# A third query block under the first norm, unread products between two blocks, and a rotation moved from TensorE to VectorE

## The chip, the cores and the metric

The kernel runs on one core of one Trainium2 chip. The core has a matrix engine (TensorE, in profiles PE, with its weight loads listed apart as PEld), two engines for elementwise work (VectorE, DVE, and ScalarE, ACT), GpSimd (POOL), and SyncE (SP), which issues most of the transfers between memory and the on-chip buffer. Products land in PSUM, which the kernel uses as eight banks of 128 x 512 numbers. The engines run side by side and wait for one another by semaphores. The metric is the time of one execution in device microseconds: the median of three runs is 2041.04 us (2039.53 to 2041.19).

## What is computed

Two transformer blocks on 256 positions of width 2048, all in float32. In outline:

```
# first block
h = rmsnorm(x, g_pre)
q, k, v, z = split(h @ w_in_a)              # 32 heads of 64, 4 key/value heads
o = sliding_window_attention(q, k, v)       # window 128, ALiBi slopes, one sink per head
y = (o * silu(z)) @ w_out_a
x = x + rmsnorm(y, g_post)
# second block
h = rmsnorm(x, attn_norm_g)
c_q, c_kv, k_pe, dq, dk, dv, gates = split(h @ w_in)
q = rmsnorm(c_q) @ w_uq                     # 16 heads: 128 plain and 64 rotated columns
k, v = split(rmsnorm(c_kv) @ w_ukv)
q_rope, k_rope = rope(q[64 columns]), rope(k_pe)
y_mla  = chunked_attention([q, q_rope], [k, k_rope], v)
y_diff = differential_attention(dq, dk, dv)
x = x + (g0 * (y_mla @ w_mla) + g1 * (y_diff @ w_diff)) @ w_out
h = rmsnorm(x, ffn_norm_g)
x = x + (silu(h @ w_gate) * (h @ w_up)) @ w_down
return rmsnorm(x, final_norm_g)
```

The rotation takes a head's 64 columns as two halves x1 and x2 and gives (x1 cos - x2 sin, x2 cos + x1 sin). A norm's factor is one number per position, so the kernel multiplies with weights first and applies the factor to the product.

## The kernel before, in words

Every activation lies with its columns on the 128 partitions and the 256 positions along the row. Each number is cut into a high part and a low part of a shorter type, and a product of a weight tile w (128 x 128) with an activation tile is formed as w_hi times [a_hi | a_lo], 512 columns in one instruction, plus w_lo times a_hi, 256 columns. `gemm(name, m, acts)` makes one block of 128 output columns this way: for 16 activation tiles it issues 8 products of one kind, 16 of the other and again 16 and 8 in turn, into one PSUM bank. `gemm4` makes four blocks together, tile by tile, into two banks of the tag "g" and two of the tag "s"; the second block's first products are made so, since each needs only one tile of h at a time. PSUM has four banks "g", two "s" and two "t".

The weights arrive as float32 chunks of 16 tiles (w_raw, four buffers); for each half chunk ACT writes the high part (line 84) and DVE the low part (line 85), into four buffers each.

The instructions of each engine run in the order in which a planner puts them ahead of time: it walks the program by priority (the order in which the code is written) and gives an engine the first instruction that its own estimate of times takes for ready, so an instruction that waits can be passed by later ones. Instructions that go through `pin` stay behind what was written before them on their engine; matrix products are not pinned.

Work of the attention and the norms is written as generators. `between.tiles(n)` counts weight tiles inside `gemm` and at each tick (after `every` tiles, there twice per block of 16) advances one generator by a step, so its products land between those of the big matrix products.

Around the change:

- First norm. The keys and values of the first block (ps_k in two "g" banks, ps_v in one of the "s" banks) and the query blocks 0 and 1 (the other two "g" banks) are formed from h before its norm is known. `first_norm` squares x_t (ACT, line 252), adds (DVE), forms the sums over partitions by products with a column of ones (`Squares.sums`), takes the root on POOL (`rstd`, line 277), and spreads the factor over partitions by a diagonal matrix times ones (`rows`, line 284); then k_a, v_a and the queries are scaled (`scaled`), which frees the banks. Its four first steps take two squares each; behind block 1 the generator is drained, that is, run to its end. Block 2 needs a "g" bank.
- Between the blocks. The last output block of `w_out_a` is made by `gemm_sum`; then its square, the sums, the root and `rows` follow one another, and nothing else is there for PE. Each tile of x1 is y times the factor plus x (lines 588 and 589, DVE), and is cut into h (lines 235 and 236) for the first `gemm4` of the second block, whose first weights were cut ahead (w_hi_u, w_lo_u).
- Rotation. `rotate(a)` forms a product of a with a constant matrix rot_m (a permutation with signs) in a "t" bank, multiplies it by sin out of PSUM, multiplies a by cos and adds. It is called once for the shared key part kr and twice in each of four groups for q_r; the scores of a group (`attend_m`) wait for it.

Of the kernel before, what the change touches and what calls it, by code (L numbers as in the profile page):

```python
# [12 lines left out]
ALU = mybir.AluOpType  # L13

P = 128
S = 256
# [10 lines left out]
N_CHUNK = N_TILES // CH  # L27

G_PRE, G_POST, G_ATTN, G_Q, G_KV, G_FFN, B_GATE, G_DIFF, N_COLS = 0, 16, 32, 48, 54, 58, 74, 106, 108
C_ID, C_ROT, C_COS, C_SIN, C_DA, C_DM, C_DD, N_CST = 0, 128, 256, 512, 768, 1152, 1536, 1920  # L30


class Weights:
# [134 lines left out]
def block_kernel(ctx, tc, order, w, xt, cols, bc, fg, cst, out):  # L168
# [10 lines left out]
    def unit(name, dt=F32):  # L179
        return up.tile([P, 512], dt, name=name, tag="u", bufs=NU)  # L180
# [4 lines left out]
    def bank(tag):  # L185
        return psum.tile([P, 512], F32, name=f"ps_{tag}", tag=tag, bufs={"g": 4, "s": 2, "t": 2}[tag])

    def half(t, i):
        return t[:, (i % 2) * S:(i % 2) * S + S]
# [78 lines left out]
    def rstd(src, dim, scale=None):  # L268
        n = src.shape[-1]
        t = sm("ms", n)  # L270
        if scale is None:
            nc.vector.tensor_scalar(out=t, in0=src, scalar1=1.0 / dim, scalar2=EPS, op0=ALU.mult, op1=ALU.add)
        else:
            nc.vector.scalar_tensor_tensor(out=t, in0=src, scalar=1.0 / dim, in1=scale, op0=ALU.mult, op1=ALU.mult)
            nc.vector.tensor_scalar(out=t, in0=t, scalar1=EPS, scalar2=None, op0=ALU.add)
        r = sm("rstd", n)
        nc.gpsimd.tensor_tensor(out=r, in0=t, in1=mhalf[:, 0:n], op=ALU.pow)  # L277
        return r

    def rows(r, rb=None):  # L280

        dg = unit("diag")[:, 0:S]
        for tb in range(2):
            nc.vector.tensor_scalar(out=dg[:, tb * P:tb * P + P], in0=ident, scalar1=r[:, tb:tb + 1], scalar2=None,
                                    op0=ALU.mult)
        ps = bank("t")
        mm(ps[:, 0:S], ones, dg, True, True)
        if rb is not None:
            nc.vector.tensor_copy(out=rb, in_=ps[:, 0:S])
        return ps[:, 0:S]  # L290
# [23 lines left out]
            between.tiles(n)  # L314
            run(same, b, opened)

    def gemm(name, m, acts):

        ps = bank("g")
        parts = [(ps, W.take(name, k * P, m * P), acts[k]) for k in range(len(acts))]  # L320
        if len(parts) > HALF:
            runs(parts[:HALF], parts[HALF:], HALF)
        else:
            runs(parts, [], len(parts))
        return ps

    def gemm4(name, ms, acts):

        pp = [bank("g"), bank("g"), bank("s"), bank("s")]
        opened = set()  # L330
        for k in range(len(acts)):
            parts = [(pp[j], W.take(name, k * P, m * P), acts[k]) for j, m in enumerate(ms)]
            same, other = ("hi", "lo") if k % 2 == 0 else ("lo", "hi")
            run(same, parts, opened)
            run(other, parts, opened)
            between.tiles(len(parts))
        return pp

    def gemm_sum(name, m, acts):

# [114 lines left out]
    def first_norm():  # L455
        for i in range(8):
            sq.add(x_t[i])
            if i % 2:
                yield
        nc.vector.tensor_copy(out=r_a, in_=rstd(sq.sums(), D))  # L460
        yield 2
        rows(r_a, rb)
        yield
        for j in range(2):
            scaled(half(k_a, j), ps_k[j], rb)
        for tb in range(2):
            nc.scalar.activation(out=half(v_a, tb), in_=half(ps_v, tb), func=AF.Copy, scale=r_a[:, tb:tb + 1])
        pin(nc.vector.tensor_scalar(out=negsink, in0=sinks, scalar1=-1.0, scalar2=None, op0=ALU.mult))

    def attend_a(j, q, o):  # L470

        kt = j // 8
        heads = (16 * kt + j % 8, 16 * kt + 8 + j % 8)
        negmax, sums, t = sm("negmax"), sm("sums"), sm("tiny")
        p = []
        pp = [bank("s") for _ in range(2)]
        for a, b, n in ((0, P, P), (P, S, S)):
            for e, ps in enumerate(pp):
                rng = slice(64 * e, 64 * e + 64)
                mm(ps[:, a:a + n], q[rng, a:b], k_a[rng, kt * S:kt * S + n], a == 0, a > 0)  # L480
        for e, ps in enumerate(pp):
            slope = 2.0 ** (-8.0 * (heads[e] + 1) / 32)
            bias = unit("bias")[:, 0:384]
            nc.scalar.activation(out=bias, in_=tab_a, func=AF.Copy, scale=8.0 * slope)
            p.append(exps(ps, bias, 0.125, negmax[:, 2 * e:2 * e + 2], sums[:, 2 * e:2 * e + 2],
                          negsink[:, heads[e]:heads[e] + 1]))
        for e in range(2):
            nc.vector.tensor_scalar(out=t[:, 2 * e:2 * e + 2], in0=negmax[:, 2 * e:2 * e + 2],
                                    scalar1=sinks[:, heads[e]:heads[e] + 1], scalar2=None, op0=ALU.add)
        nc.scalar.activation(out=t, in_=t, func=AF.Exp)  # L490
        rec = sm("rec")
        tt(rec, t, sums, ALU.add)
        nc.vector.reciprocal(out=rec, in_=rec)
        for e in range(2):
            nc.scalar.activation(out=p[e][:, 0:P], in_=p[e][:, 0:P], func=AF.Copy, scale=rec[:, 2 * e:2 * e + 1])
            nc.vector.tensor_scalar(out=p[e][:, P:384], in0=p[e][:, P:384], scalar1=rec[:, 2 * e + 1:2 * e + 2],  # L496
                                    scalar2=None, op0=ALU.mult)
        yield
        pts = [transposed(p[e], e == 1) for e in range(2)]
        yield  # L500
        ps = bank("t")
        vs = [v_a[:, tb * S + (2 * kt + e) * 64:tb * S + (2 * kt + e) * 64 + 64] for e in range(2) for tb in range(2)]
        for e in range(2):
            mm(ps[64 * e:64 * e + 64, 0:S], vs[2 * e], pts[e][:, 0:S], True, False)
        for e in range(2):
            mm(ps[64 * e:64 * e + 64, P:S], vs[2 * e + 1], pts[e][:, S:384], False, True)
        nc.scalar.copy(out=o, in_=ps[:, 0:S])
        done.add(j)
# [2 lines left out]
    between.every, between.apart = 4, 1  # L511
    between.add(first_norm())
    o_a = []
    for j in range(16):
        ps = gemm("in_a", j, h)
        if j == 0:
            ps_0 = ps
            continue
        if j == 1:
            between.drain()  # L520
            between.every, between.apart = 8, 3
        for i, b in ((0, ps_0), (1, ps)) if j == 1 else ((j, ps),):
            if i % 2 == 0:
                q, o = unit("q_a"), unit("o_a")
                o_a.append(o)
            scaled(half(q, i), b, rb)
            between.add(attend_a(i, half(q, i), half(o, i)))

    lam = unit("lam")
    nc.gpsimd.dma_start(out=lam, in_=bc[:, 32:544])  # L530
# [45 lines left out]
                      [(unit("w_hi_u", F32R), unit("w_lo_u", F32R)) for _ in range(2)])  # L576
    ps = gemm_sum("out_a", 15, g)
    sq.add(ps[:, 0:S])
    rb = rows(rstd(sq.sums(), D))
    t = half(y2[7], 1)  # L580
    nc.scalar.activation(out=t, in_=ps[:, 0:S], func=AF.Copy, scale=gcol(G_POST, 15))
    y.append(t)
# [21 lines left out]
    rope = unit("rope")  # L604
    nc.scalar.dma_start(out=rope, in_=cst[:, C_COS:C_COS + 512])
    cos, sin = rope[:, 0:S], rope[:, S:]
    rot_m = unit("rot_m")
    rot, tab_m = rot_m[:, 384:512], rot_m[:, 0:384]
    nc.scalar.dma_start(out=rot, in_=cst[:, C_ROT:C_ROT + P])
    nc.scalar.dma_start(out=tab_m, in_=cst[:, C_DM:C_DM + 384])  # L610

    r_2 = const.tile([P, 2], F32, name="r_2")
# [32 lines left out]

    def rotate(a):

        ps = bank("t")
        mm(ps[:, 0:S], rot, a, True, True)
        b = unit("rope_t")[:, 0:S]  # L650
        tt(b, ps[:, 0:S], sin, ALU.mult)
        tt(a, a, cos, ALU.mult)
        tt(a, a, b, ALU.add)

# [325 lines left out]
def _constants():  # L980
    c = np.zeros((P, N_CST), np.float32)
    c[:, C_ID:C_ID + P] = np.eye(P)
    for b in (0, 64):
        for i in range(32):
            c[b + 32 + i, C_ROT + b + i] = -1.0
            c[b + i, C_ROT + b + 32 + i] = 1.0
    inv = np.float32(10000.0) ** (-np.arange(0, 64, 2, dtype=np.float32) / np.float32(64))
    ang = (np.arange(S, dtype=np.float32)[:, None] * inv[None, :]).astype(np.float32)
    for b in range(4):
        c[b * 32:b * 32 + 32, C_COS:C_COS + S] = np.cos(ang).T  # L990
        c[b * 32:b * 32 + 32, C_SIN:C_SIN + S] = np.sin(ang).T
    q = np.arange(P)[:, None]
    k = np.arange(S)[None, :]
    for q0, o, n in ((0, 0, P), (P, P, S)):
        qq, kk = q + q0, k[:, :n]
        dist = qq - kk
        c[:, C_DA + o:C_DA + o + n] = np.where((dist >= 0) & (dist < 128), -dist, -1e30)
        ok = kk // 64 <= qq // 64
        c[:, C_DM + o:C_DM + o + n] = np.where(ok, 0.0, -1e30)
        c[:, C_DD + o:C_DD + o + n] = np.where(ok, -np.abs(dist), -1e30)  # L1000
    return c
# [69 lines left out]
```

## Time and profile before

| | |
|---|---|
| median of three runs | 2041.04 us |
| the profiled execution's own time | 2042.15 us |
| span, first to last instruction | 2040.4 us |
| mean granted TensorE clock | 0.996 |
| PE busy | 2014.4 us (99%) |
| DVE, ACT busy | 1304.3 us (64%), 1071.6 us (53%) |
| moved from and to memory | 364.89 MB, 179 GB/s |

The profile is of one execution. Busy is the time in which an engine executes something; for PE matrix products overlap, so one instruction's length is more than its share of the stream: 16 products of 512 columns follow one another in 3.65 us, though each is listed with about 0.39. A row of a timeline gives start, length, engine, line, what is written and read, and in brackets how long the engine stood idle before it and who released it. "The chain" follows the execution back from its last instruction; in it the lengths add up to the span.

### The profile page before, as it was taken

The page shows a single profiled execution, that of the slowest core. Times are in us where ns is not written, and L with a number is a line of the kernel's source. Part 1 is how long each engine was busy: PE and PEld are TensorE (multiplying, and loading weights), DVE is VectorE, ACT ScalarE, POOL GpSimd, SP SyncE. Part 2 cuts the span into 40 slices and gives each one's busy share as a digit, 9 for nine tenths or more (in the row PEclk, how much of TensorE's full clock was granted, in tenths as well). Part 3 has the DMA queues.
Part 4 walks back from the last instruction along what each step waited for, and adds up shares of the span by engine and source line. Part 5 has one row for each costly group of instructions (what it writes and reads, how often), then busy time and mean ns, then how long its engine had stood idle before and what let it go on. Part 6 is the DMA issues. An engine that isn't in the chain of part 4 may idle for free.

```text
span 2040.4 us, 28289 instructions
## 1 busy us (share of the span) xinstructions
PE 2014.4 (99%) x11290; PEld 1744.5 (85%) x11290; DVE 1304.3 (64%) x2129; ACT 1071.6 (53%) x1818; POOL 19.2 (1%) x25
## 2 busy tenths in 40 slices
PE   7999999999999999999999999999999999999998
PEld 6787888888888888888888888888888888888886
DVE  6768865887766655566575767666666666555543
ACT  6767655656545444455465445464445554444443
POOL 0000000000000000000000000000000000000000
PEclk9999999999999999999999999999999999999999
DMA  7343456353444555545545555545555555555553
GB/s 295 119 152 128 166 186 232 109 186 125 149 159 171 186 186 187 193 171 174 183 166 186 187 193 193 185 173 187 189 193 194 187 186 187 191 220 186 196 196 103
DMA packets 53667, 364.89 MB, mean 179 GB/s; under 512 B 6240, under 2 KB 7136, under 8 KB 10400
## 3 DMA queue, kind: packets, MB, share of 16 engines
q1 hardware_dynamic: 52560, 361.07, 49.5%
q8 instruction: 88, 1.44, 0.3%
q0 software_dynamic: 400, 1.31, 0.2%
q10 hardware_dynamic: 576, 0.72, 0.1%
q14 instruction: 43, 0.35, 0.1%
HBM read 360.98 MB, written 2.10 MB: 178 GB/s over the span
## 4 chain that ended last, share of the span: by engine, by line
PE 96%; DVE 1%; ACT 1%; issue 1%; DMA 0%; SPq 0%; POOL 0%; POOLq 0%; ACTq 0%; DVEq 0%
PE ps_g L195 89%; PE ps_s L195 5%; PE ps_t L195 2%; PE ps_t L412 1%; DMA w_raw<-w 0%; ACT prob L404 0%; DVE w_lo L85 0%; ACT w_hi L84 0%; PE ps_t L810 0%; PE ps_t L906 0%; POOL rstd L277 0%; PE ps_t L786 0%; DVE prob L400 0%; DVE prob L496 0%; SPq L217 0%
## 5 line engine op out<-in xcount | busy, mean ns | idle before, releaser
L85 DVE TENSOR_TENSOR w_lo<-w_raw,w_hi 128x1024 fp32r<-128x1024 f32 (+1 forms) x676 | 825.6, 1222 | 320.0 <-ACT w_hi L84 289.9
L84 ACT CAST w_hi<-w_raw 128x1024 fp32r<-128x1024 f32 (+1 forms) x676 | 708.3, 1048 | 352.7 <-PE ps_g L195 269.6
L195 PE MATMUL ps_g<-h,w_hi 128*128 128x512 f32 x3064 | 750.1, 393 | 8.1 <-ACT w_hi L84 6.7
L195 PEld LDWEIGHTS ps_g<-h,w_hi 128*128 128x128 f32 x3064 | 561.9, 189 | 120.2 <-ACT w_hi L84 6.7
L195 PEld LDWEIGHTS ps_g<-h,w_lo 128*128 128x128 f32 x3064 | 395.2, 191 | 20.3 <-issue 4.0
L195 PE MATMUL ps_g<-h,w_lo 128*128 128x256 f32 x3064 | 408.4, 284 | 0.9 <-DVE k_a L198 0.9
L195 PE MATMUL ps_g<-w_hi,act 128*128 128x512 f32 x704 | 216.8, 389 | 0.0
L195 PEld LDWEIGHTS ps_g<-w_hi,act 128*128 128x128 f32 x704 | 132.1, 188 | 27.5
L381 ACT COPY ffn<-ps_g 128x256 f32<-128x256 f32 x86 | 31.8, 373 | 200.9 <-PE ps_g L195 200.9
L195 PE MATMUL ps_g<-w_lo,act 128*128 128x512 f32 x352 | 136.9, 389 | 0.0
L198 DVE TENSOR_TENSOR ffn<-ffn,ps_g 128x256 f32<-128x256 f32 x86 | 36.0, 421 | 144.4 <-ACT ffn L381 144.4
L195 PE MATMUL ps_g<-w_hi,h 128*128 128x512 f32 x256 | 79.4, 389 | 0.0
L195 PEld LDWEIGHTS ps_g<-w_lo,act 128*128 128x128 f32 x352 | 66.1, 188 | 13.7
L404 ACT ACTIVATE prob<-prob,negmax 128x128 f32<-128x128 f32 (+1 forms) x128 | 56.7, 445 | 24.1 <-DVE negmax L400 23.5
L195 PE MATMUL ps_g<-y_m,w_hi 128*128 128x512 f32 x256 | 63.8, 391 | 0.0
L195 PE MATMUL ps_g<-y_d,w_hi 128*128 128x512 f32 x256 | 61.2, 391 | 0.0
L195 PE MATMUL ps_g<-g,w_hi 128*128 128x512 f32 (+1 forms) x240 | 57.8, 377 | 0.0
L195 PEld LDWEIGHTS ps_g<-w_hi,h 128*128 128x128 f32 x256 | 48.1, 188 | 9.9
L195 PE MATMUL ps_g<-mg,w_hi 128*128 128x512 f32 x224 | 56.0, 391 | 0.0
L195 PEld LDWEIGHTS ps_g<-y_d,w_hi 128*128 128x128 f32 x256 | 47.0, 188 | 9.1
L195 PEld LDWEIGHTS ps_g<-y_m,w_hi 128*128 128x128 f32 x256 | 47.0, 188 | 9.1
L195 PE MATMUL ps_g<-c,w_hi 128*128 128x512 f32 x208 | 53.6, 400 | 0.0
(238 smaller groups left out, 1859.2 us busy)
## 6 DMA issues: line engine op xcount, KB each, us to landing
w_raw<-w SPq DMA_DIRECT2D x337, 1024.0 KB, 4.8
w_raw<-w SPq DMA_DIRECT2D x5, 512.0 KB, 7.8
out<-x2n SPq DMA_DIRECT2D x8, 256.0 KB, 3.1
x_t<-xt SPq DMA_DIRECT2D x7, 256.0 KB, 7.8
fgt<-fg POOLq DMA_DIRECT2D x4, 256.0 KB, 5.5
w_raw<-w SPq DMA_DIRECT2D x2, 256.0 KB, 4.6
x_t<-xt SPq DMA_DIRECT2D x2, 128.0 KB, 3.2
lam<-bc POOLq DMA_DIRECT2D x1, 256.0 KB, 6.1
```

The source lines that it names most:

```text
L84: a = nc.scalar.copy(out=hi[:, q], in_=src[:, q])
L85: b = nc.vector.tensor_tensor(out=lo[:, q], in0=src[:, q], in1=hi.bitcast(F32)[:, q], op=ALU.subtract)
L195: nc.tensor.matmul(out=o, lhsT=a, rhs=b, start=start, stop=stop, skip_group_check=True)
L198: nc.vector.tensor_tensor(out=o, in0=a, in1=b, op=op)
L381: nc.scalar.copy(out=o, in_=ps[:, S:])
L404: nc.scalar.activation(out=t[:, a:b], in_=t[:, a:b], func=AF.Exp, scale=-1.0, bias=negmax[:, qb:qb + 1], accum_out=sums[:, qb:qb + 1])
L412: nc.tensor.transpose(out=ps[:, j * P:j * P + P], in_=p[:, j * P:j * P + P], identity=ident)
```

## The change

Three edits.

- The first norm's generator takes four squares per step instead of two, and the loop over query blocks makes block 2 as well before draining it; block 2 is written into an "s" bank. All three blocks are scaled, and their attention queued, behind block 2.
- `busy(n, cols)` issues n products of g[0] with itself, cols columns wide, into an "s" bank that nothing reads. It is called three times between the blocks: 8 of 128 columns after the sums, 2 of 256 after the root, 8 of 512 after `rows`.
- `rotate` uses no product: for each group of 32 partitions, DVE multiplies a by sin and writes the result to the neighbouring group (q ^ 32). The sign of the rotation is in the table of sin, the matrix rot_m and its load are gone.

```
     def first_norm():
         for i in range(8):
             sq.add(x_t[i])
-            if i % 2:
+            if i % 4 == 3:
                 yield
...
+    early = []
     for j in range(16):
-        ps = gemm("in_a", j, h)
-        if j == 0:
-            ps_0 = ps
+        ps = gemm("in_a", j, h, "s" if j == 2 else "g")
+        early.append((j, ps))
+        if j < 2:
             continue
-        if j == 1:
+        if j == 2:
             between.drain()
             between.every, between.apart = 8, 3
-        for i, b in ((0, ps_0), (1, ps)) if j == 1 else ((j, ps),):
+        for i, b in early:
             if i % 2 == 0:
                 q, o = unit("q_a"), unit("o_a")
                 o_a.append(o)
             scaled(half(q, i), b, rb)
             between.add(attend_a(i, half(q, i), half(o, i)))
+        early = []
...
+    def busy(n, cols):
+
+        ps = bank("s")
+        for _ in range(n):
+            mm(ps[:, 0:cols], g[0][:, 0:P], g[0][:, 0:cols], True, True)
...
     sq.add(ps[:, 0:S])
-    rb = rows(rstd(sq.sums(), D))
+    sums = sq.sums()
+    busy(8, P)
+    r = rstd(sums, D)
+    busy(2, S)
+    rb = rows(r)
+    busy(8, 512)
...
-    rot_m = unit("rot_m")
-    rot, tab_m = rot_m[:, 384:512], rot_m[:, 0:384]
-    nc.scalar.dma_start(out=rot, in_=cst[:, C_ROT:C_ROT + P])
+    tab_m = unit("tab_m")[:, 0:384]
...
     def rotate(a):
 
-        ps = bank("t")
-        mm(ps[:, 0:S], rot, a, True, True)
         b = unit("rope_t")[:, 0:S]
-        tt(b, ps[:, 0:S], sin, ALU.mult)
+        for q in range(0, P, 32):
+            tt(b[q ^ 32:(q ^ 32) + 32], a[q:q + 32], sin[q:q + 32], ALU.mult)
         tt(a, a, cos, ALU.mult)
         tt(a, a, b, ALU.add)
...
-        c[b * 32:b * 32 + 32, C_SIN:C_SIN + S] = np.sin(ang).T
+        c[b * 32:b * 32 + 32, C_SIN:C_SIN + S] = np.sin(ang).T * (1.0 if b % 2 == 0 else -1.0)
```

More of the change, by code (lines that the diff above doesn't have):

```diff
@@ L29 @@
 G_PRE, G_POST, G_ATTN, G_Q, G_KV, G_FFN, B_GATE, G_DIFF, N_COLS = 0, 16, 32, 48, 54, 58, 74, 106, 108
-C_ID, C_ROT, C_COS, C_SIN, C_DA, C_DM, C_DD, N_CST = 0, 128, 256, 512, 768, 1152, 1536, 1920
+C_ID, C_COS, C_SIN, C_DA, C_DM, C_DD, N_CST = 0, 128, 384, 640, 1024, 1408, 1792
 class Weights:
@@ L315, in runs, with gemm @@
             run(same, b, opened)
-    def gemm(name, m, acts):
-        ps = bank("g")
+    def gemm(name, m, acts, tag="g"):
+        ps = bank(tag)
         parts = [(ps, W.take(name, k * P, m * P), acts[k]) for k in range(len(acts))]
@@ L982, in _constants @@
     c[:, C_ID:C_ID + P] = np.eye(P)
[L983 to L986, printed above, removed]
     inv = np.float32(10000.0) ** (-np.arange(0, 64, 2, dtype=np.float32) / np.float32(64))
```

## The prediction

> **What bounds the kernel now.** I read the page's busy times first, then PE's share of the waits, then a table of busy time by stretch, and last the instructions around the places where PE stands still.
>
> ```profile
> PE 2014.4 (99%) x11290; PEld 1744.5 (85%) x11290; DVE 1304.3 (64%) x2129; ACT 1071.6 (53%) x1818; POOL 19.2 (1%) x25
> ```
>
> PE is the bound: 26 us of the span of 2040.4 are not PE's. So only two kinds of edit pay: work taken off PE, and the few waits of PE shortened. Its waits behind other engines, apart from the start, are these:
>
> ```profile
> PE ps_t L195 <- DVE diag L284: 4.3, 2, 2.7
> PE ps_g L195 <- DVE h L236: 3.7, 2, 2.2
> PE ps_g L195 <- DVE k_a L198: 0.9, 1, 0.9
> ```
>
> The stretches that the change touches (columns: length, then busy us and instructions of PE, PEld, DVE, ACT, POOL, then the granted clock, DMA share, GB/s):
>
> ```profile
> 33.50:50.00 16.50, 12.90 (x75) 11.15 (x74) 11.06 (x18) 8.02 (x13) 1.54 (x1) 0.99 0.63 235
> 50.00:75.00 25.00, 24.42 (x147) 19.76 (x147) 18.66 (x61) 17.20 (x49) 0.00 (x0) 0.94 0.26 96
> 75.00:200.00 125.00, 124.68 (x770) 99.28 (x769) 87.98 (x246) 85.53 (x222) 0.70 (x1) 1.00 0.41 146
> 352.00:368.00 16.00, 11.97 (x58) 10.09 (x57) 9.47 (x27) 4.59 (x10) 0.72 (x1) 0.68 0.11 33
> 395.00:450.00 55.00, 55.00 (x311) 48.06 (x310) 46.22 (x95) 34.64 (x66) 2.91 (x3) 1.00 0.50 180
> 450.00:600.00 150.00, 150.00 (x877) 128.44 (x876) 111.50 (x253) 85.03 (x188) 0.00 (x0) 1.00 0.41 146
> ```
>
> The reader is to see two holes of PE (16.50 - 12.90 = 3.6 us and 16.00 - 11.97 = 4.0 us), each with a granted clock below 1 in or behind it, and no hole at all in the two stretches where the rotations lie.
>
> **First norm: the third query block.** PE's own instructions there (start, length, what; in brackets the idle time before):
>
> ```profile
> 40.04 3.82 PE L195 MATMUL ps_g<-h,w_hi 128*128 128x512 f32 x16
> 43.69 1.12 PE L195 MATMUL ps_g<-h,w_lo 128*128 128x256 f32 x8
> 44.65 0.50 PE L195 MATMUL ps_t<-ones,sq 128*128 128x1 f32 x4
> 47.81 0.70 PE L195 MATMUL ps_t<-diag,ones 128*128 128x256 f32 x2 [2.66 <-DVE diag L284]
> 49.45 1.86 PE L195 MATMUL ps_g<-h,w_lo 128*128 128x256 f32 x8 [0.94 <-DVE k_a L198]
> 51.10 2.46 PE L195 MATMUL ps_g<-h,w_hi 128*128 128x512 f32 x6
> 53.50 0.93 PE L195 MATMUL ps_s<-k_a,q_a 64*128 64x128 f32 x8
> ```
>
> Blocks 0 and 1 end at 44.65; then sums, root, diagonal and k_a must finish before block 2 gets a ps_g bank. That is 2.66 + 0.94 = 3.6 us of idle. Behind it PE runs slow: 8 low-half products take 51.10 - 49.45 = 1.65 us against 44.65 - 43.69 = 0.96 before, and 6 high-half ones 53.50 - 51.10 = 2.40 against 6 x (43.69 - 40.04)/16 = 1.37. That is 0.69 + 1.03 = 1.7 us lost to the clock, so 5.3 us in all.
>
> With the change, sums fall a quarter into block 1 (about 40), rows a quarter into block 2 (about 46), k_a at its third quarter. Block 2 writes a ps_s bank, which is free because ps_v holds only one of two, and runs 5.6 us (3.65 + 2 x 0.96) through what was the hole. The chain from sums to rows was 47.81 - 44.65 = 3.2 us, against the two ticks of 2.8 us, half a block, that it now has, so it is hidden; k_a's adds free the ps_g bank before block 3 asks for it. Moved with it: the squares are two per tick more, on ACT and DVE, which are busy 8.0 and 11.1 of 16.5 us here. The first attention now starts one block later with three heads' pairs queued instead of two, and waits for block 2's own scaling to free its second ps_s bank, much as it waited four us (49.45 to 53.50) before. No DMA is moved past another. I take -5.2; bounds -3.6 (the idle alone, the clock falls elsewhere) and -5.5.
>
> **Between the blocks: products nobody reads.**
>
> ```profile
> 354.75 1.24 PE L195 MATMUL ps_t<-ones,sq 128*128 128x1 f32 x8
> 357.64 1.22 PE L195 MATMUL ps_t<-diag,ones 128*128 128x256 f32 x2 [1.65 <-DVE diag L284]
> 361.11 1.19 PE L195 MATMUL ps_g<-h,w_hi_u 128*128 128x512 f32 x2 [2.25 <-DVE h L236]
> ```
> ```profile
> 368.29 0.24 PE ps_g L195 x2
> 371.07 0.24 PE ps_g L195 x2
> 382.25 0.24 PE ps_g L195 x2
> ```
> ```profile
> 379.23 0.48 DVE L236 SCALAR_TENSOR_TENSOR h<-y,colt,h 128x256 fp32r<-128x256 f32 x1
> ```
>
> The first fence is PE's timeline, the second the chain that ended last. The rows product takes 1.22 us where the first norm's took 0.70: the clock is already down. The first three k steps of the new block take 368.29 - 361.11 = 7.18 us; two later ones take 371.07 - 368.29 = 2.78, so three cost 4.17 at full clock: 3.0 us lost, of which I leave 0.3 for filling the pipe.
>
> The change adds, on PE alone, 8 products of 128 columns before the root, 2 of 256 behind it, 8 of 512 behind rows. A 256-column one costs 0.12 (0.96/8), a 512-column one 0.23 (3.65/16). A 128-column one of this type is not in the trace; 4 products of one column took 0.50, so the bounds are 0.12 and the 0.23 of four times the width, and I take 0.12, the nearer row by shape. So 1.0 + 0.24 us fit the gap of 1.65 before rows, and 1.8 the gap of 2.25 behind it. Nobody reads their bank, so nothing waits for them except PE's own next instruction.
>
> If the clock holds, rows takes 0.5 less and everything behind it moves up; and of the 2.7 us behind 361.11 nearly all returns. What is late next: h. Block 13 of h is done at 379.23 + 0.48 and PE begins that step at 382.25, a slack of 2.5 us; PE gains 3.2 on it while DVE gains 0.5, so some 0.2 to 0.4 of the gain is lost there. 0.5 + 2.3 = 2.8; I take off 0.3 because what holds the dummies in place is only the planner:
>
> ```profile
> L817 DVE TENSOR_SCALAR hb<-colt x1: 175/175/175, 3.3 to 3.3; 128x32 f32<-128x32 f32 x1
> ```
>
> This instruction of line 817 ran at 3.3 us: work that is ready is issued early when its engine looks free. I take -2.5; bounds -3.3 and +1.5 (rival 1).
>
> [...]
>
> **Rotation on DVE.** Removed: a product per rotation, and a 64 KB load on ACT's queue. Added: four multiplies of 32 partitions for one of 128.
>
> ```profile
> 454.17 0.87 PE ps_t L195 x4
> ```
> ```profile
> 358.90 0.42 DVE L588 TENSOR_TENSOR y<-y,ps_t 128x256 f32<-128x256 f32 x1 [1.31 <-PE ps_t L195]
> 359.35 0.42 DVE L589 TENSOR_TENSOR y<-y,x_t 128x256 f32<-128x256 f32 x1
> 359.69 0.41 DVE L588 TENSOR_TENSOR y<-y,ps_t 128x256 f32<-128x256 f32 x1
> ```
> ```profile
> 454.01 1.03 PE L195 MATMUL ps_t<-q_r,rot_m 128*128 128x256 f32 x4
> 455.91 0.42 DVE L198 TENSOR_TENSOR rope_t<-ps_t,rope 128x256 f32<-128x256 f32 x1
> 458.25 0.42 DVE L198 TENSOR_TENSOR q_r<-q_r,rope_t 128x256 f32<-128x256 f32 x1
> 459.08 0.93 PE L195 MATMUL ps_s<-rb_kr,q_r 64*128 64x128 f32 x8
> ```
> ```profile
> 490.01 1.03 PE L195 MATMUL ps_t<-q_r,rot_m 128*128 128x256 f32 x4
> 491.37 0.42 DVE L198 TENSOR_TENSOR rope_t<-ps_t,rope 128x256 f32<-128x256 f32 x1
> 493.71 0.42 DVE L198 TENSOR_TENSOR q_r<-q_r,rope_t 128x256 f32<-128x256 f32 x1
> 495.94 0.93 PE L195 MATMUL ps_s<-rb_kr,q_r 64*128 64x128 f32 x8
> ```
>
> Two rotations hold PE 0.87 us, so nine hold it 9 x 0.435 = 3.9, in stretches where PE has no hole: a gain one for one. A multiply of 32 partitions is not in the trace; it streams the same 256 elements per partition as the 0.42 us rows, which I take (bounds 0.1, a quarter, and 0.45, the start-to-start of a dependent pair, 358.90 to 359.35; an independent one follows after 0.34). Three more at 0.42 are 1.26 per rotation, 11.3 for nine. Cover: DVE idles 55.00 - 46.22 + 150.00 - 111.50 = 47.3 us there. What could be late is q_r for the scores. A group of two rotations gets 2.5 us longer on DVE, but need not wait for PE, behind whose start rope_t began 1.9 and 1.4 us later. In the first group q_r was done 459.08 - 458.67 = 0.4 us ahead of the scores, in the second 1.8 us: late by 0.2, and not at all. I allow 0.4 for all four and take -3.5; bounds -3.9 and rival 3. The load removed leaves ACT's queue where ACT waits for DVE anyway, 4.11 us as its next row has it: nothing.
>
> ```profile
> 359.81 0.51 ACT L235 ACTIVATE h<-y,colt 128x256 fp32r<-128x256 f32 x1 [4.11 <-DVE y L589]
> ```
>
> [...]
>
> **Sum.** -5.2 - 2.5 - 3.5 = -11.2 us against the profiled execution's own time of 2042.15 (span 2040.4 and 1.75 around it), so 2031.0. The median of the runs, 2041.04, lies 1.1 below that execution: 2029.8, so 2030. By the bounds the same case reaches from -12.7 to -8.0: 2028 to 2033. About 0.2%, 4.1 us, is what a measurement of this kernel can tell from no change.
>
> **Rivals.** (1) The dummies don't do it. Either the planner issues all eighteen ahead of rows: 1.0 + 0.24 + 1.8 = 3.0 us into the 1.65 us hole makes rows 1.4 late, and the hole behind it stays; or the clock falls all the same, and the eight wide ones at twice 0.23 fill 3.7 us where 2.25 were free, 1.4 late too; or the planner puts them into busy PE time earlier, +3.0. Then this part is +1.4 to +3.0 instead of -2.5: 2033.7 to 2035.3. For it: the row of line 817. Against: ahead of 354.75 PE has no idle place to tempt the planner. (2) The first norm's wait only moves, behind block 2, to the attention's ps_s banks: 5.2 are lost, 2035. For it: scores started 4.0 us after block 2 did. Against: block 3 needs no ps_s bank and can run meanwhile. (3) The other side: q_r comes late in the four groups and DVE becomes what PE waits for. The place is the scores; the price is up to 2.5 us per group, and from 1.65 us on (the shortest hole behind which the clock was down) 3.0 more for the clock. In all four: 4 x 5.5 = 22 us for the rotation's gain, -7.7 - 3.9 + 22 = +10.4, 2051. In two of four: 2040.4, no change. For it: the first group's slack of 0.4 us. Against: the 47 us of idle DVE, and that PE's order lets other products pass the scores, as at 51.10 where six went ahead.
>
> **How the numbers follow.** Forecast 0.58; rival 1 0.2; rival 2 0.07; rival 3 in two groups 0.08, in all 0.07. The first three are faster: 0.85; the others 0.08 the same and 0.07 slower. From 2027.5 (the bound, with the spread of the runs) to 2036.5 lie the first three.
>
> **What would show it.** After the change PE should wait for no diagonal and no k_a near 45 to 50; the granted clock of the first 75 us should be 1; rows between the blocks should take 0.70, and its k steps 1.39 from the first on. No ps_t product from rot_m, 36 DVE multiplies of 32 partitions at about 0.42, and scores right behind. I am wrong if the stretch from the sums to the first k step grows beyond its 6.4 us, if PE's busy share in the rotation stretches falls below all, or if the dummies stand somewhere else.

## The result and the profile after

The changed kernel took 2034.28 us (median; 2033.72 to 2036.05) against 2040.80 us for the kernel before on the same chip: a ratio of 0.997 [0.9961, 0.998], 6.5 us less. The profiled execution took 2034.21 us with a span of 2032.4, 8.0 less than the span before; the profiled execution of before (2042.15) had lain 1.35 us above the median of 2040.80, which is most of the difference between 8.0 and 6.5.

PE is busy for 2010.5 us after, DVE for 1316.0. The waits of PE in the changed kernel (what waited, at what, behind whom: us in total, times, the longest):

```profile
...
PE ps_g L195 <- DVE k_n L198: 1.8, 2, 1.4
PE ps_t L418 <- ACT prob_t L421: 0.8, 1, 0.8
PE ps_s L195 <- DVE negmax L406: 0.7, 2, 0.4
PE ps_t L195 <- DVE diag L284: 0.6, 1, 0.6
PE ps_s L195 <- DVE q_r L198: 0.5, 1, 0.5
```

The wait for k_a is gone and that for the diagonals has shrunk from 4.3 to 0.6 us, as forecast. But waits for k_n, prob_t, negmax and q_r have come up, 3.8 us together. Of these 0.3 us, for negmax at 161 us, lie in the first block, where the kernel before had short waits for prob_t and q_a; the other 3.5 are in the second block and new there. The table by stretch (length, then busy us and count of PE, PEld, DVE, ACT, POOL, then clock, DMA share, GB/s) says where:

```profile
33.50:50.00 16.50, 16.50 (x96) 14.48 (x95) 12.95 (x24) 7.95 (x13) 0.70 (x1) 1.00 0.65 238
50.00:75.00 25.00, 25.00 (x158) 20.57 (x158) 20.02 (x60) 19.36 (x53) 0.00 (x0) 1.00 0.35 131
...
395.00:450.00 55.00, 53.46 (x303) 46.55 (x303) 45.42 (x92) 31.09 (x53) 2.91 (x3) 1.00 0.50 184
450.00:600.00 150.00, 147.86 (x859) 125.47 (x858) 119.55 (x273) 84.08 (x186) 0.00 (x0) 1.00 0.41 144
```

The first hole is closed, at full clock. In the two stretches of the rotations, where PE had no hole before, it now stands still for 1.54 + 2.14 = 3.7 us. PE's timeline at the first norm shows the new order, sums and rows inside blocks 1 and 2, with no idle time ahead of any of them:

```profile
39.41 0.50 PE L195 MATMUL ps_t<-ones,sq 128*128 128x1 f32 x4
...
45.44 0.59 PE L195 MATMUL ps_t<-diag,ones 128*128 128x256 f32 x2
45.68 4.00 PE L195 MATMUL ps_s<-h,w_hi 128*128 128x512 f32 x16
```

and between the blocks:

```profile
349.45 0.50 PE L195 MATMUL ps_t<-ones,sq 128*128 128x1 f32 x4
349.81 0.42 PE L195 MATMUL ps_s<-g 128*128 128x128 f32 x2
...
350.55 1.15 PE L195 MATMUL ps_s<-g 128*128 128x128 f32 x8
352.34 0.70 PE L195 MATMUL ps_t<-diag,ones 128*128 128x256 f32 x2 [0.64 <-DVE diag L284]
352.69 2.20 PE L195 MATMUL ps_s<-g 128*128 128x512 f32 x8
355.20 0.73 PE L195 MATMUL ps_g<-h,w_hi_u 128*128 128x512 f32 x2 [0.31 <-DVE h L236]
```

The 18 unread products stand where they were written (two slipped between the sums; the row of eight at 350.55 is the other six of 128 columns and the two of 256), rows is back at 0.70 us, and the first pair of k-step products takes 0.73 where it took 1.19. The first query block's first products are needed as a mark too, before and after:

```profile
33.51 1.12 PE L195 MATMUL ps_g<-h,w_lo 128*128 128x256 f32 x8
```
```profile
32.88 1.12 PE L195 MATMUL ps_g<-h,w_lo 128*128 128x256 f32 x8
```

The last output's transfers serve as the end mark. They start on SP's queue, before and after:

```profile
2028.80 7.23 SPq L973 DMA_DIRECT2D out<-x2n  x8
```
```profile
2021.30 7.21 SPq L983 DMA_DIRECT2D out<-x2n  x8
```

These marks split the gain. Up to the first query block: 33.51 to 32.88, -0.6; this is start-up and no part of the change (PE leaves its last start-up wait at 15.12 before and 14.49 after). From there to the sums between the blocks: 354.75 - 33.51 = 321.24 to 349.45 - 32.88 = 316.57, -4.7 (first norm). Sums to the first k step: 361.11 - 354.75 = 6.36 to 355.20 - 349.45 = 5.75, -0.6 (mostly rows). From the first k step to the transfers: 1667.7 to 1666.1, -1.6. From there to the end the span shrank by another 0.5, which the runs did not look into. The -1.6 is the disappointment: it should hold the clock's gain for the k steps, about 2.3, and the rotation's 3.5.

The instructions in which PE resumes after an idle time in the rotation stretches:

```profile
426.10 0.48 PE L195 MATMUL ps_g<-w_hi,c 128*128 128x512 f32 x1 [1.41 <-DVE k_n L198]
...
453.22 0.50 PE L195 MATMUL ps_g<-w_hi,c 128*128 128x512 f32 x1 [0.44 <-DVE k_n L198]
...
454.23 0.93 PE L195 MATMUL ps_s<-rb_kr,q_r 64*128 64x128 f32 x8 [0.50 <-DVE q_r L198]
...
503.12 1.02 PE L418 MATMUL ps_t<-ident,prob 128*128 128x128 f32 x6 [0.83 <-ACT prob_t L421]
...
527.53 1.58 PE L195 MATMUL ps_s<-k_n,q_n 128*128 128x128 f32 x8 [0.37 <-DVE negmax L406]
```

Only one of the five waits is for a rotated tile q_r. What delays the longest is told by the chain of that stretch:

```profile
423.80 0.42 DVE rope_t L198
...
424.22 0.41 DVE rope_t L198
...
424.65 0.42 DVE rope_t L198
...
425.08 0.42 DVE rope_t L198
...
425.53 0.42 DVE k_n L198
```

The four multiplies of kr's rotation run on DVE immediately ahead of the k_n that empties a "g" bank, and PE waits for that k_n with its next product into a "g" bank. How that stood with the product is seen in the first experiment.

### The profile page after: what moved, and what is told of

Read it like the earlier page. It is cut to its first block, busy times and chain, and to the rows that moved or that the text cites. A ratio compares the mean times of both kernels' runs of the same rounds, so it can differ in the third digit from the quotient of the medians.

```text
span 2032.4 us, 28308 instructions
## 1 busy us (share of the span) xinstructions
PE 2010.5 (99%) x11290; PEld 1740.7 (86%) x11290; DVE 1316.0 (65%) x2156; ACT 1071.9 (53%) x1818; POOL 18.3 (1%) x25
## 4 chain that ended last, share of the span: by engine, by line
PE 95%; DVE 2%; ACT 1%; DMA 1%; issue 1%; POOL 0%; SPq 0%; ACTq 0%; POOLq 0%; DVEq 0%
PE ps_g L195 87%; PE ps_s L195 5%; PE ps_t L195 2%; PE ps_t L418 1%; DMA w_raw<-w 1%; DVE rope_t L198 1%; DVE w_lo L85 1%; DVE k_n L198 0%; ACT w_hi L84 0%; DVE q_r L198 0%; DVE prob L406 0%; PE ps_t L916 0%; PE ps_t L820 0%; POOL rstd L277 0%; PE ps_t L796 0%
```

## Experiments

The kernels start from the changed one unless it is said otherwise, and all compute the whole result. Beside each median stands its ratio to the kernel before, timed in the same job. "The stretch" is from the first k step to the last output's transfers: 1667.7 us before, 1666.1 changed.

**Undo the rotation.**

```
-        for q in range(0, P, 32):
-            tt(b[q ^ 32:(q ^ 32) + 32], a[q:q + 32], sin[q:q + 32], ALU.mult)
+        ps = bank("t")
+        mm(ps[:, 0:S], rot, a, True, True)
+        tt(b, ps[:, 0:S], sin, ALU.mult)
```

> The changed kernel with one part undone: the rotation is a product with rot_m on PE again. Theory T, from the two traces: the rotation on DVE took 3.9 us of products off PE and gave back more in waits, about 1.1 us net, so this kernel takes 2034.3 - 1.1 = 2033.2 us. Rival R, the prediction's own term: the rotation gained 3.5 us and the shortfall lies in another part, so 2037.8 us.

2033.88 us, 0.9962 [0.995, 0.9975]; 0.4 below the changed kernel by the medians, within what the intervals allow, and 1.1 by the stretch, 355.47 to 2020.45 = 1665.0. The table by stretch shows PE without a hole again:

```profile
395.00:450.00 55.00, 55.00 (x313) 48.18 (x312) 45.72 (x93) 31.60 (x53) 2.91 (x3) 1.00 0.53 191
450.00:600.00 150.00, 150.00 (x873) 128.28 (x872) 109.31 (x245) 83.98 (x185) 0.00 (x0) 1.00 0.40 142
```

DVE's timeline at kr, with the product:

```profile
423.96 0.42 DVE L198 TENSOR_TENSOR rope_t<-ps_t,rope 128x256 f32<-128x256 f32 x1
...
424.62 0.41 DVE L198 TENSOR_TENSOR k_n<-k_n,ps_g 128x256 f32<-128x256 f32 x1
```

The rotation stood ahead of k_n here too, but k_n starts 0.66 us after rope_t; in the chain of the changed kernel it is 425.53 - 423.80 = 1.73, and PE, with a product less to make, comes for the bank earlier. So the rotation on DVE, as placed, brought nothing and by the profile cost 1.1 us; with the product back the stretch is 2.7 shorter than before, and since the rotations are then as before, that is put down to the clock in the k steps.

**Undo the unread products.**

```
-    sums = sq.sums()
-    busy(8, P)
-    r = rstd(sums, D)
-    busy(2, S)
-    rb = rows(r)
-    busy(8, 512)
+    rb = rows(rstd(sq.sums(), D))
```

> The changed kernel without the eighteen unread products. Theory T: between the end of the last output block and the fourth k step of the second block the changed kernel is 3.3 to 3.5 us shorter, and that is the granted clock, so without the products the clock is down again behind the gap and the time is 2037.7 us, with a rows product of 1.2 us. [...]

2036.5 us, 0.9975 [0.9965, 0.9986]: 2.2 more than the changed kernel, 2.1 by the stretch (355.21 to 2023.38 = 1668.2). PE's timeline and the table by stretch:

```profile
352.26 0.70 PE L195 MATMUL ps_t<-diag,ones 128*128 128x256 f32 x2 [1.65 <-DVE diag L284]
355.21 1.19 PE L195 MATMUL ps_g<-h,w_hi_u 128*128 128x512 f32 x2 [2.25 <-DVE h L236]
```
```profile
352.00:354.00 2.00, 0.70 (x2) 0.30 (x2) 1.17 (x5) 0.09 (x1) 0.00 (x0) 0.71 0.12 45
354.00:356.00 2.00, 0.79 (x2) 0.72 (x3) 1.93 (x6) 1.04 (x3) 0.00 (x0) 0.50 0.00 0
356.00:358.00 2.00, 2.00 (x8) 1.71 (x8) 1.93 (x6) 0.91 (x2) 0.00 (x0) 0.50 0.00 0
358.00:360.00 2.00, 2.00 (x9) 1.77 (x9) 1.97 (x6) 1.02 (x2) 0.00 (x0) 0.58 0.00 0
```

The same two holes as before the change, and the clock falls, but later against the work: rows runs at 0.70, and only the k steps are slow. Of the 3.3 us that this boundary gained in the profiles (0.6 + 2.7), the unread products hold 2.1; the other 1.2 is there without them, in this profile and with the boundary some 5 us earlier than before the change.

**Undo the third block.** Two blocks ahead of the drain, two squares per step, block 2 in a "g" bank.

```
-            if i % 4 == 3:
+            if i % 2:
...
-        ps = gemm("in_a", j, h, "s" if j == 2 else "g")
+        ps = gemm("in_a", j, h)
...
-        if j < 2:
+        if j < 1:
             continue
-        if j == 2:
+        if j == 1:
```

> The changed kernel with two query blocks before the first norm is drained and two squares per step, as before. Theory T: the last output block of the first transformer block ended 5.3 us earlier with three blocks, and all of it is kept, so 2039.6 us. Rival: a part of it is given back behind, where three heads' pairs of attention start together; then 2037 us or less.

2039.04 us, 0.9988 [0.998, 0.9997]: 4.8 more than the changed kernel, 4.9 by the span of 2037.3. The hole is the old one (PE is busy for 12.90 of the 16.50 us from 33.50 on), and the clock is down to 0.50 behind it (50 to 52 us). From the first query block, at 33.12, to the sums, at 354.36, it takes 321.24 us, as in the kernel before; so the third block is worth 4.7.

This kernel also shows the unread products at nearly the old place of the boundary:

```profile
357.25 0.70 PE L195 MATMUL ps_t<-diag,ones 128*128 128x256 f32 x2 [0.63 <-DVE diag L284]
```

The kernel before, with its sums at 354.75 and no such products, had 1.22 for this row. From the sums to the first k step (360.11) it is 5.75 us here, and the stretch is 2026.15 - 360.11 = 1666.0, both as in the changed kernel. Against the kernel before that is 0.6 + 1.7, and with the 1.1 that the rotation costs, 3.4: in this place the products are worth all that the boundary gained, against 2.1 in the other. Each is one execution, so whether the place or the way the low clock happened to fall made the difference is open.

By the medians the three undone parts are worth 4.8, 2.2 and -0.4 us: 6.6 together, where 6.5 was measured. This fit is in part luck. The products' worth is not the same in each place, and the kernel before ran 0.7 us slower in the job of these three than in the first (2041.54 and 2040.80); measured against it the parts are 4.0, 1.5 and -1.1.

**Only kr by a product, q_r on DVE.**

```
+        if product:
+            ps = bank("t")
+            mm(ps[:, 0:S], rot, a, True, True)
+            tt(b, ps[:, 0:S], sin, ALU.mult)
+        else:
...
-        rotate(kr)
+        rotate(kr, True)
```

> The changed kernel with only the rotation of kr done by a product on PE, the eight of q_r on DVE. Theory T: kr's four multiplies stand ahead of the k_n that frees a bank, and PE waited 1.4 us for it; the product costs PE 0.4, so 2034.3 - 1.0 = 2033.3 us, and no wait of PE for k_n near 426 us. Rival: the loss is with the q_r groups alone, kr's wait only moves; then 2034.7 us.

2034.04 us, 0.9965 [0.9952, 0.9979]. Its five times spread from 2032.97 to 2035.77, so the median tells little. In the profile the stretch is 1664.6 (355.25 to 2019.84), 1.5 less than changed, and of PE's two waits for k_n only the short one, 0.4 us, is left.

So by the profiles kr alone cost what the eight rotations of q_r gained (0.4 against the first experiment), and more.

**The changed kernel again**, beside the next three kernels on their chip.

> The changed kernel, unaltered, beside the next three on one chip. Expected: its own time, 0.997 of before, 6.5 us less.

2034.39 us, 0.9968 [0.9955, 0.998]; stretch 2021.46 - 355.40 = 1666.1. The two marks lie 0.2 us later than in the first profile, and the stretch repeats to 0.1 us.

**kr on DVE, but later:** the same multiplies, behind the first group's k_n and values. (Two empty steps of the norms' generator go with it.)

```
         yield from fin_kv()
-        yield
-        yield
-        rotate(kr)
...
             between.drain()
             between.every, between.apart = 5, 4
+            rotate(kr)
```

> The changed kernel with one step moved: kr is rotated on DVE after the first group's k_n and values are out of their banks, not between the key norm's factor and k_n. Theory T: what kr's rotation costs is its place ahead of k_n, not its length; PE's wait of 1.4 us near 426 us goes and nothing takes its place, since kr is first read some 25 us later: 1.5 us less than the changed kernel. Rival: DVE is the bound in this stretch, so twelve DVE instructions cost the same wherever they stand, and the wait only moves: no gain.

2032.56 us, 0.9957 [0.9945, 0.997]; the stretch is 1664.3 (355.00 to 2019.30), 1.8 less than changed. No instruction was taken away, only the place was changed: the four multiplies are as long as they were (0.42 us), and the 1.41 us wait is gone. Their length cost something only where they stood.

**And q_r earlier:** besides, each group's first rotation is written right behind q_r and the second two ticks on.

```
     def rope_q(u, qr):
-        yield
-        for i in range(2):
-            rotate(half(qr, i))
+        rotate(half(qr, 0))
+        yield 2
+        rotate(half(qr, 1))
```

> As the run with kr late, and each group's two rotations begin at the first tick after q_r, one per tick with one tick between, not both together four ticks later. Theory T: q_r is late because both rotations stand together just ahead of the scores; spread out they use DVE's idle time and the waits of about 2.1 us left in the groups go: 1.5 us less than with kr late alone, 3 less than the changed kernel. Rival: they now push back the scaling of q_n that frees banks, as kr pushed back k_n: no gain or a loss of 1 us.

2031.23 us, 0.9947 [0.9934, 0.9961]; stretch 1662.0 (356.32 to 2018.33), 4.1 less than changed and 3.0 less than with the product. (The first k step is late here, as shown below; the last experiment has the same rotations and an early first k step, and its stretch is 1662.1.) The waits for k_n, q_r and prob_t are gone, and PE has one stop left in the two stretches (0.55 us, for a w_lo):

```profile
395.00:450.00 55.00, 54.45 (x309) 46.57 (x307) 48.75 (x111) 31.37 (x61) 2.07 (x3) 1.00 0.47 171
450.00:600.00 150.00, 150.00 (x871) 128.56 (x870) 117.95 (x258) 85.27 (x182) 0.00 (x0) 1.00 0.42 150
```

DVE is about as busy as in the changed kernel (48.75 + 117.95 = 166.7 us over both stretches against 45.42 + 119.55 = 165.0). The waits for prob_t and negmax, which are steps of the softmax, went with the wait for q_r; the 0.3 us for negmax in the first block stays, as it does with the product. So these too hung on where the rotation stood in DVE's order: in the changed kernel the addition that ends one (526.50) runs immediately ahead of the softmax's first instruction (526.84), for whose end PE waits at 527.53. In this profile, though, the boundary went differently:

```profile
352.33 1.21 PE L195 MATMUL ps_t<-diag,ones 128*128 128x256 f32 x2 [0.64 <-DVE diag L284]
352.98 3.51 PE L195 MATMUL ps_s<-g 128*128 128x512 f32 x8
356.32 0.62 PE L195 MATMUL ps_g<-h,w_hi_u 128*128 128x512 f32 x2
```
```profile
352.00:354.00 2.00, 1.67 (x4) 1.39 (x5) 0.69 (x3) 0.00 (x0) 0.00 (x0) 0.59 0.15 55
354.00:356.00 2.00, 2.00 (x6) 1.55 (x6) 1.91 (x5) 1.01 (x2) 0.00 (x0) 0.55 0.00 0
```

The clock fell in spite of the same unread products, and the eight wide ones took 3.51 us for 2.20 and made the first k step 1.1 us late; behind them it is 1.00 again. That is the second form of the prediction's first rival, in one execution. This kernel's five times reach from 2029.79 to 2032.04.

**The four multiplies on GpSimd**, everything else as in the last kernel.

```
-            tt(b[q ^ 32:(q ^ 32) + 32], a[q:q + 32], sin[q:q + 32], ALU.mult)
+            nc.gpsimd.tensor_tensor(out=b[q ^ 32:(q ^ 32) + 32], in0=a[q:q + 32], in1=sin[q:q + 32], op=ALU.mult)
```

> As the run before, with the four multiplies of each rotation on GpSimd, which is idle 99% of the span. Theory T: DVE then has two instructions per rotation where the kernel of old had three, and PE none, so the whole 3.9 us of products is kept: 4 us less than the changed kernel. Rival: GpSimd is slow at it or holds up DVE at the memory they share, q_r comes later than now and DVE's last two instructions wait in front of the weights' split: 0 to 8 us more than the changed kernel.

2033.42 us, 0.9959 [0.9947, 0.9972], 2.2 more than on DVE. POOL's groups by line, and DVE's waits:

```profile
L661 POOL TENSOR_TENSOR rope_t<-q_r,rope 32x256 f32<-32x256 f32 x32 | 31.4, 980 | 77.4 <-DVE q_r L198 70.8 <-ACT w_hi L84 3.2 <-PE ps_g L195 0.9
```
```profile
DVE q_r L198 <- POOL rope_t L661: 7.0, 4, 2.7
```

A multiply takes 980 ns on average there for 420 on DVE, and DVE's q_r waits for it four times, 7.0 us. Some of DVE's own instructions grew beside it too: the longest addition that ends a rotation takes 0.84 us, where all eight took 0.42 in the changed kernel; what held it up the trace does not show. PE in turn waits 2.4 us for q_n, which DVE makes as well. The time, 1.0 less than the changed kernel, lies between the two expectations. An idle engine was no better place.

**Only the wide unread products, behind rows** (from the changed kernel).

```
     sums = sq.sums()
-    busy(8, P)
     r = rstd(sums, D)
-    busy(2, S)
     rb = rows(r)
     busy(8, 512)
```

> The changed kernel with only the last eight wide dummies of the boundary (behind the rows); the ten narrow ones ahead of the rows are left out, nothing else. [...] Theory B (it is the last gap before the k steps alone that brings the clock down): the late dummies hold everything, 2034.3, and the first k step is at 0.70. Rival (the ten narrow ones carry the gain): as without dummies, 2036.5.

2035.67 us, 0.9973 [0.9962, 0.9984], with a wide spread (2034.09 to 2038.08), 1.4 more than the changed kernel. The edit did not give what it says:

```profile
350.42 1.42 PE L195 MATMUL ps_s<-g 128*128 128x512 f32 x5
352.21 0.70 PE L195 MATMUL ps_t<-diag,ones 128*128 128x256 f32 x2 [0.37 <-DVE diag L284]
...
355.15 0.70 PE L195 MATMUL ps_g<-h,w_hi_u 128*128 128x512 f32 x2 [2.02 <-DVE h L236]
```

The planner moved seven of the eight wide products ahead of rows (two of them, not shown, between the sums), into the hole that the narrow ones had filled. So it was the narrow products that had kept the wide ones in place, and this run could not tell which gap matters. Still, in this profiled execution, the fastest of its runs, the clock held through 2.02 us of idle PE (1.00 in every row from 348 to 370 us); the spread of the times suggests that in others it did not.

**Only the narrow ones, ahead of rows.**

```
     busy(2, S)
     rb = rows(r)
-    busy(8, 512)
```

> The changed kernel with only the ten narrow dummies ahead of the rows; the eight wide ones behind the rows are left out. PE then stands still some 2.2 us between the rows and the first k step. [...] Theory B: nothing holds the last gap; as without dummies, 2036.5, with the first k steps at 1.2 us instead of 0.70. Rival: the narrow ones carry the gain, 2034.3 and k steps at 0.70.

2035.81 us, 0.9977 [0.9968, 0.9987]: 1.5 more than the changed kernel and 0.7 less than without any, though the single times overlap (2035.41 to 2037.55 here, 2035.87 to 2036.92 without). In the profile the first k step takes 1.19 us behind 2.25 us of idle time, and the clock of the six us from 354 on is

```profile
354.00:356.00 2.00, 1.03 (x3) 0.87 (x4) 1.97 (x6) 1.04 (x3) 0.00 (x0) 0.71 0.00 0
356.00:358.00 2.00, 2.00 (x9) 1.81 (x8) 1.93 (x7) 0.66 (x2) 0.00 (x0) 0.50 0.00 0
358.00:360.00 2.00, 2.00 (x11) 1.71 (x10) 1.93 (x6) 1.02 (x2) 0.00 (x0) 0.94 0.00 0
```

By the medians neither set alone, as the planner placed it, gives the changed kernel's time; the intervals of the ratios overlap, so how much each holds is open.

**Six wide products in place of the eight narrow ones**, from the best kernel (kr late, q_r early).

```
     sums = sq.sums()
-    busy(8, P)
+    busy(6, 512)
     r = rstd(sums, D)
```

> The best version so far (kr rotated late, each q_r early; 2031.23) with the first eight narrow dummies of 128 columns replaced by six of 512 (about 1.65 us for 1.15), which end just as the rows can start. If what brought the clock down in that version's profile (rows at 1.21, late dummies 3.51 for 2.20, the first k step 1.1 us late) was the 0.64 us of PE still idle ahead of the rows and the thin work beside it, the rows come at 0.70, the late dummies at 2.2, and the time is 2030.1 to 2031.2. [...] If the longer dummies hold up the rows, 2031.5 to 2032.

2030.41 us, 0.9948 [0.9933, 0.9963], its four times between 2030.06 and 2030.58. In its profile rows takes 0.70 again, 0.36 us of PE is idle ahead of it, and

```profile
352.97 2.20 PE L195 MATMUL ps_s<-g 128*128 128x512 f32 x8
355.49 0.73 PE L195 MATMUL ps_g<-h,w_hi_u 128*128 128x512 f32 x2 [0.31 <-DVE h L236]
```

The expected case, though the 0.8 us between this and the kernel with eight narrow products lie inside the intervals, that kernel's times lie on both sides of these four, and one profile cannot show that the clock never falls. By the median it is the fastest version here, 10.5 us below the kernel before.

## Why the prediction was right, and where it was not

The time lies in the range and on the forecast side, 4.3 us above the number of 2030. One of the three terms, the rotation, carries that. It was luck for this term that the range held: it reaches to 2036.5 for the sake of rivals 1 and 2, and neither came. Two of the recorded figures do not add up, though nothing hangs on them: the weak end of the same case, -8.0, is not to be had from the bounds given (-3.6 - 2.5 - 3.5 = -9.6), and the bound of +1.5 between the blocks is less than the +3.0 of rival 1 for the same part. And 1.5 of the 3.7 us listed for h lie in the start-up.

**First norm.** The term was -5.2; measured from the first query block to the sums between the blocks it is -4.7, and undoing the part costs 4.8 by the medians. Where the missing half us went was not looked into. All its steps are in the profile: sums at 39.4, rows at 45.4, no wait for a diagonal or k_a, clock 1 up to 75 us. Rival 2 falls: the first scores start at 51.53 with no idle PE ahead of them.

**Between the blocks.** The term was -2.5, with -3.3 as its bound. The profiles show -3.3, the bound; undoing the products costs only 2.1 to 2.2. The mechanism was right (rows back to 0.70, the first k step at 0.73, 18 products where they were written). "If the clock holds, rows takes 0.5 less" is borne out at the old place of the boundary, where rows took 1.22 without the products and 0.70 with them (third block undone, 3.4 for the whole part); at the new place rows took 0.70 without them too. So in these profiles what the products are worth depended on where the low clock fell, and the forecast had one number for it. What it took off for a late h was not needed: PE has no idle time from the first k step to 395 us. The price of a product of 128 columns came out as taken: in the row of six such and two of 256, 1.15 us long with 0.28 for the last, one starts every 0.12 us. Of rival 1, the planner's move did not happen to the changed kernel, but it did when the narrow products were left out; the clock that falls all the same was seen once, in a kernel with the same products at the boundary.

**Rotation.** This is the term that failed: -3.5 forecast, +1.1 by the stretch and +0.4 by the medians. The prediction's own sign of being wrong came up here: PE's busy share in the rotation stretches fell below all. Not its instructions: no rot_m product is left, and a multiply of 32 partitions takes the 0.42 us that was assumed. Not the size of the gain either: with better places the same rotation gains 2.9 to 3.0 over the product. The step that failed is the cover, 47.3 us of idle DVE, and the sentence "What could be late is q_r for the scores." Idle time summed over 205 us hides nothing by itself, and q_r was only one of the things that DVE owes PE. The waits that came up were for a bank (k_n, 1.41 and 0.44), for the softmax (prob_t 0.83, negmax 0.37) and for q_r (0.50): 3.55 in the five rows, 3.7 by the table. And kr's rotation, counted as one of nine with no place of its own, was the dearest of them: 1.5 us by the profile when it went back to a product, 1.8 when it was only moved. Rival 3 had the direction, DVE as what PE waits for, and named the wrong place; its price of 2.5 us per group and the fall of the clock behind it did not come: the stops are 1.41 us at most, and the clock stays at 1.00 in both stretches.

The sum of idle time still leaves a rest. Against the kernel with the product, the changed one should gain 3.9 - 3.7 = 0.2 and loses 1.1. The kernel with kr late has 2.13 us of idle PE in four stops and gains 0.7; the best one has 0.55 in one stop and gains 2.9 (1665.0 - 1662.1). Idle time and gain add up to 2.6, 2.8 and 3.4 us at five, four and one stops: an estimate that fits all three is 3.65 us for the nine products, and 0.2 for each stop beside its idle time. The kernel with only kr by a product, which the fit left out, agrees: eight ninths of 3.65, less 2.15 us of idle time and four stops, is 0.3, and it gains 0.4. The rows do not decide it: the product behind a stop takes 0.48 or 0.50 where its neighbours take 0.39, but the one of 426.10 takes 0.48 in the first experiment too (425.24), with no stop ahead of it; these are single profiles, and no run separated this.

With the rotation placed (and six wide products for the eight narrow ones), the three terms give nearly what was forecast: 10.5 us below the kernel before, where the sum was 11.2.

## What to carry to other kernels

Work that is moved to an engine with idle time needs a place in that engine's queue: before pricing it at nothing, list what the bounding engine next needs from that queue (banks freed, softmax pieces, operands), and see which of the moved instructions will stand ahead of those. The same instructions in another place made 3.2 us of difference here by the medians. And a filler for the clock must stay where it is meant to be. Undo it on its own, in more than one place of the boundary if that can be had: here the profiles put it at 2.1 us in one and 3.4 in the other.

## What the runs showed of the hardware

**The low clock lasted about 3.4 us, or two or three times that.** The lowest clock in any row is 0.50 (in the kernel before from 50 to 52 us and from 358 to 366). If it is only ever 0.50 or 1, a stretch's low time is twice its length times what its clock lacks of 1. By this estimate it is 1.64 + 1.80 = 3.4 us for the kernel with q_r early, 1.16 + 2.00 + 0.24 = 3.4 with the narrow products alone, 1.16 + 2.00 + 2.00 + 1.68 = 6.8 with none, and 16.00 x 0.32 x 2 = 10.2 between the blocks of the kernel before: one, one, two and three times 3.4, in one execution each. What brings the clock down the runs did not settle. Taken as one piece, the low time of the kernel with q_r early ended by 355.8 (354 plus 1.80), so it began at 352.4, and the 3.4 us ahead of that held 0.4 us of the last block's products, then sums and unread products with 0.64 us of idle PE. In the kernel before, the clock is 1.00 up to 356.80 and 0.57 in the 0.4 us behind it, and the 3.4 us ahead of that held 1.3 us of the last block's products, the 1.24 us of one-column products and 0.9 us of idle PE. With the wide products alone the clock stayed at 1.00 through 2.02 us of idle PE. In the execution with q_r early the low time fell mostly on the wide products, and the k steps ran at a clock of 1.00; whether the products ended it is not shown, since with the narrow ones alone it also lasted 3.4 us.

**The four multiplies on different partitions followed one another more slowly.** kr's four start 0.42 us apart (423.80, 424.22, 424.65, 425.08), each behind the end of the one before, while of two independent instructions on 128 partitions the second started 0.34 us after the first, in the forecast's rows (359.35 and 359.69) and right behind kr's four (k_n at 425.53, kr times cos at 425.87). What made the difference no run separated. Four multiplies of a quarter so took 4 x 0.42 = 1.7 us of DVE, and cutting the partitions saved nothing here: one on 32 of them took 0.42 us, as one on 128 did.
